# Second feed-forward of a two-layer trunk: norm and first weight tiles by token blocks of 128, with up to seven raw weight buffers

## The chip, the cores and the metric

The kernel runs on one core of a Trainium2 chip. The time is the device time of one execution in microseconds; of several runs the median is given. The engines are named as the profile names them: PE (matrix products), DVE (vector), ACT (scalar, activations), POOL (general) and SP, whose queue issues most DMAs.

## What is computed

A backbone of two layers over 256 latent tokens and 256 context tokens, 1024 features each, in float32. Layer 0 mixes tokens with an mLSTM, layer 1 with latent attention; each is followed by a gated feed-forward with a convolution over three tokens. The part around the change, for the latent tokens of layer 1, comes down to

```python
y  = attention(...) @ a_w_out                        # 256 x 1024
x3 = layer_norm(ALPHA * x2 + gate2 * y)              # per token, then * g + b
h  = x3 * (1 + scale4) + shift3
gate, up = split(h @ w_in, 2)                        # w_in: 1024 x 5632
act = silu(dwconv3(gate, conv_w) + conv_b) * up      # conv along tokens
out = layer_norm(ALPHA * x3 + gate5 * (act @ w_out))
```

## The kernel before, in words

**Arithmetic.** Each float32 operand is split into a high part in the reduced format fp32r and a low part that is the rest. A product is three matmuls (`mm3`, lines 313 to 315): high by high, high by low, low by high, summed in PSUM.

**Weights.** All weights lie in DRAM as tiles of 128 x 1024 in the order of their use (`_plan`). The class `Stream` brings them: `_load` (line 236) issues one DMA on SP's queue into a raw buffer, `_split` (line 244) makes the two parts, the cast on ACT (L257) and the subtraction on DVE (L258). There are NRAW = 3 raw buffers: a tile is loaded when an earlier one has been split. The parts go into one of NB = 3 `w` buffers ("narrow") or, for tiles marked wide, into two of the 31 buffers of 4 KB per partition of tag `u`, which activations share. `use` hands out the next tile and splits up to 8 ahead, as far as buffers and `limit` allow; `pump` raises the limit by hand; with `hold=True` a tile is kept until `unhold`.

**Order.** The Tile framework puts every operation on its engine in an order fixed before the run. The order of the code is its priority; an operation that is ready earlier by the framework's estimate may be placed ahead of others. Background work (norms) is written as generators, stepped by `tick` and finished by `drain`.

**Stages around the change.** `mla` (line 1252) computes the attention head by head and pumps the tiles of the attention output meanwhile. `outmm("aout")` multiplies the eight tiles of a_w_out; by `TAIL` the last seven are held, and the tail runs group by group: for token block 0 two groups of 512 columns, for block 1 one of 512 and two of 256 (`acc4(True)`). Then `after0` norms both blocks: `ln_rows` (L953, L954, L956 to L963, L982 to L985) makes `z`, one block after the other; `ln_T` (line 1003) transposes both blocks of `z` on PE (L1011), applies scale and shift (L1018, L1020) and splits the result into `h1` (L1023, L1024). `ln_x` later finishes x3 on DVE (L1039, L1040) and stores it for the last residual; its rows `gr` and `br` are broadcast by POOL.

`ffn_in` (line 1104) takes 22 pairs of tiles, a gate and an up tile of 128 columns of w_in each. The weights are stationary, and the 256 tokens move: 24 matmuls of 256 columns per tile. The convolution, SiLU, product and split of a pair follow (L598 to L605, L1129 to L1132). In layer 1 the first two pairs (`fin1` 0 and 1) are wide, and `pump` with QA, QB, QC = 2, 4, 6 splits them during the norm. `outmm("fout1")` with ten wide tiles and the last norm end the program.

The tags `acc` and `ar`, two buffers of 128 x 1024 each, serve the modulation vectors (L440) earlier; `ar` also holds the rope tables in the attention. The tag `s2`, 13 buffers of 128 x 512, holds residuals, gates, broadcast rows, softmax rows and small temporaries.

## Time and profile before

| what | value |
|---|---|
| median of 3 runs | 1431.02 us (1429.1 to 1434.94) |
| profiled execution | 1429.89 us, its span 1428.1 us |
| DVE, ACT busy | 980.5 us, 642.3 us |
| raw weight loads (L240, SP) | x300, 512 KB each, median 3.9 us from issue to landing |
| attention output's wide tiles on PE | 1198.8 to 1220.9 us |
| second feed-forward's first 22 pairs on PE | 1229.8 to 1357.5 us |
| granted PE clock, mean of the span | 0.996 |

All times inside the execution are counted from the span's start. The page gives each engine's busy time and share; groups of instructions by line of code; and waits, where an idle stretch of an engine is put down to whatever released it. A matmul's listed duration includes its pipeline, so the distance between starts tells what it costs. The window view gives, for a stretch of time, the busy time of each engine, the clock granted to PE (1.00 is full), the share of the DMA engines and the bytes they moved.

### The profile page before, as it was taken

The page shows a single profiled execution, that of the slowest core. Times are in us where ns is not written, and L with a number is a line of the kernel's source. Part 1 is how long each engine was busy: PE and PEld are TensorE (multiplying, and loading weights), DVE is VectorE, ACT ScalarE, POOL GpSimd, SP SyncE. Part 2 cuts the span into 40 slices and gives each one's busy share as a digit, 9 for nine tenths or more (in the row PEclk, how much of TensorE's full clock was granted, in tenths as well). Part 3 has the DMA queues.
Part 4 walks back from the last instruction along what each step waited for, and adds up shares of the span by engine and source line. Part 5 has one row for each costly group of instructions (what it writes and reads, how often), then busy time and mean ns, then how long its engine had stood idle before and what let it go on. Part 6 is the DMA issues. An engine that isn't in the chain of part 4 may idle for free.

```text
span 1428.1 us, 18819 instructions
## 1 busy us (share of the span) xinstructions
PE 1398.6 (98%) x7095; PEld 1176.5 (82%) x7095; DVE 980.5 (69%) x1437; ACT 642.3 (45%) x972; POOL 100.1 (7%) x185
## 2 busy tenths in 40 slices
PE   7999999999999999999999999999999999899997
PEld 3788888888888888888888888888887998899986
DVE  6696778885775666666787444444567888777755
ACT  6554231224334254464553333334364665555542
POOL 0010110003001010210001000000000001000000
PEclk9999999999999999999999999999999999999999
DMA  9475776777774745555635333335666315367763
GB/s 335 172 240 185 238 250 220 253 232 269 252 230 154 221 136 173 178 178 179 207 129 193 91 116 116 121 123 171 191 187 208 122 53 183 124 187 216 223 198 102
DMA packets 82827, 262.70 MB, mean 184 GB/s; under 512 B 11352, under 2 KB 19752, under 8 KB 82736
## 3 DMA queue, kind: packets, MB, share of 16 engines
q1 hardware_dynamic: 68304, 214.82, 48.2%
q0 software_dynamic: 14144, 46.17, 9.6%
q8 instruction: 55, 0.90, 0.3%
q10 hardware_dynamic: 288, 0.52, 0.1%
q14 instruction: 36, 0.29, 0.1%
HBM read 243.56 MB, written 17.91 MB: 183 GB/s over the span
## 4 chain that ended last, share of the span: by engine, by line
PE 65%; issue 18%; DMA 6%; DVE 6%; ACT 3%; POOL 2%; SPq 0%; DVEq 0%; POOLq 0%; ACTq 0%
PE fin L315 8%; PE fin L313 8%; PE fin L314 8%; PE y L314 5%; PE y L315 5%; PE y L313 5%; PE qk L315 4%; PE qk L313 4%; PE qk L314 4%; DMA raw<-in_ws 3%; DMA ar<-in_ada_w 2%; DVE wu L258 1%; PE up L313 1%; DMA xcr<-xcd 1%; PE up L315 1%
## 5 line engine op out<-in xcount | busy, mean ns | idle before, releaser
L258 DVE TENSOR_TENSOR w<-raw,w 128x1024 fp32r<-128x1024 f32 (+2 forms) x267 | 323.9, 1213 | 240.2 <-ACT w L257 239.7
L257 ACT CAST w<-raw 128x1024 fp32r<-128x1024 f32 (+2 forms) x267 | 278.6, 1045 | 437.2 <-PE tok L315 153.3
L315 PE MATMUL fin<-h,w 128*128 128x256 f32 (+1 forms) x696 | 231.6, 333 | 0.5 <-DVE w L258 0.5
L314 PE MATMUL fin<-h,w 128*128 128x256 f32 (+1 forms) x696 | 231.8, 333 | 0.0
L313 PE MATMUL fin<-h,w 128*128 128x256 f32 (+1 forms) x696 | 231.7, 334 | 0.0
L440 DVE SCALAR_TENSOR_TENSOR acc<-ar,cond,acc 128x1024 f32<-128x1024 f32 x112 | 140.6, 1279 | 36.0 <-DMA ar<-in_ada_w 35.6
L315 PEld LDWEIGHTS fin<-h,w 128*128 128x128 f32 x696 | 132.2, 190 | 13.8 <-DVE w L258 0.9
L314 PEld LDWEIGHTS fin<-h,w 128*128 128x128 f32 x696 | 132.2, 190 | 13.0 <-DVE h L1024 0.2
L313 PEld LDWEIGHTS fin<-h,w 128*128 128x128 f32 x696 | 132.0, 190 | 12.8
L313 PE MATMUL qk<-xc,w 128*128 128x512 f32 x256 | 101.1, 395 | 0.0
L313 PE MATMUL tok<-w,xm 128*128 128x512 f32 x256 | 100.4, 392 | 0.0
L315 PE MATMUL qk<-xc,w 128*128 128x512 f32 x256 | 100.1, 391 | 0.2 <-DVE w L258 0.2
L314 PE MATMUL qk<-xc,w 128*128 128x512 f32 x256 | 99.9, 390 | 0.0
L315 PE MATMUL tok<-w,xm 128*128 128x512 f32 x256 | 99.7, 389 | 0.0
L314 PE MATMUL tok<-w,xm 128*128 128x512 f32 x256 | 99.6, 389 | 0.0
L313 PE MATMUL y<-w,act 128*128 128x512 f32 (+1 forms) x212 | 80.4, 379 | 0.0
L315 PE MATMUL y<-w,act 128*128 128x512 f32 (+1 forms) x212 | 80.1, 378 | 0.0
L314 PE MATMUL y<-w,act 128*128 128x512 f32 (+1 forms) x212 | 80.1, 378 | 0.0
L258 DVE TENSOR_TENSOR wu<-raw,wu 128x1024 fp32r<-128x1024 f32 x36 | 43.9, 1222 | 21.7 <-ACT wu L257 21.3
L315 PEld LDWEIGHTS qk<-xc,w 128*128 128x128 f32 x256 | 48.1, 188 | 10.6 <-DVE w L258 0.6
L313 PEld LDWEIGHTS tok<-w,xm 128*128 128x128 f32 x256 | 48.0, 188 | 10.3
L315 PEld LDWEIGHTS tok<-w,xm 128*128 128x128 f32 x256 | 48.1, 188 | 10.1
(357 smaller groups left out, 2756.6 us busy)
## 6 DMA issues: line engine op xcount, KB each, us to landing
raw<-in_ws SPq DMA_DIRECT2D x300, 512.0 KB, 3.9
ar<-in_ada_w SPq DMA_DIRECT2D x80, 512.0 KB, 4.5
adaw<-in_ada_w SPq DMA_DIRECT2D x32, 256.0 KB, 6.5
xcd<-cv POOLq DMA_DIRECT2D x16, 256.0 KB, 3.2
od<-o POOLq DMA_DIRECT2D x16, 256.0 KB, 4.0
vd<-v POOLq DMA_DIRECT2D x16, 256.0 KB, 3.9
xcr<-xcd POOLq DMA_DIRECT2D x16, 256.0 KB, 6.7
vr<-vd POOLq DMA_DIRECT2D x16, 256.0 KB, 3.8
```

Source lines behind the costliest of these rows:

```text
L257: k.nc.scalar.copy(h[:, :cols], raw[:, :cols])
L258: k.nc.vector.tensor_sub(l[:, :cols], raw[:, :cols], h[:, :cols])
L313: mm(out, w[0], x[0], start=start, stop=False)
L314: mm(out, w[0], x[1], start=False, stop=False)
L315: mm(out, w[1], x[0], start=False, stop=stop)
L440: nc.vector.scalar_tensor_tensor(acc[j], w, s, acc[j], op0=ALU.mult, op1=ALU.add)
```

## The change

It has three parts. The four tiles of the first two pairs of layer 1 are packed another way (`fin1m`): 256 of the 1024 rows of w_in, by the 512 columns of both gate and both up tiles, so that they are the moving operand. Two of them are narrow, two wide.

The norm goes by token blocks of 128. Block 0's `ln_rows` is emitted after its last group of the attention output (`each`, called in `outmm`'s tail), its transposes and scale-and-shift (`ln_T1`) after the first group of block 1. When the attention output is done, block 1 is normed in `ln_rows`; block 0 is multiplied with the four tiles (`ffn_rows`: 24 matmuls of 512 columns, the tokens stationary); then follow block 1's `ln_T1` and its 24 matmuls. The results lie in token rows; `ffn_cols` copies them to SBUF and transposes them back, so that pairs 0 and 1 go on as before. From pair 2 on, `ffn_in` is unchanged. The residual and the gate of this norm are loaded from within `mla`, at head 6.

Raw buffers: the `Stream` keeps a ring of tags. It has the three `raw` buffers at first, from the first `fout0` tile on also the two of `acc` (five), and from the first `aout` tile on also the two of `ar` (seven); as many tiles are loaded ahead.

```diff
@@ _plan
-    for p in range(NF):
-        add(("fin1", p, 0), 1024, p < 2)
-        add(("fin1", p, 1), 1024, p < 2)
+    for c in range(4):
+        add(("fin1m", 0, c), 1024, c >= 2)
+    for p in range(2, NF):
+        add(("fin1", p, 0), 1024)
+        add(("fin1", p, 1), 1024)
@@ _pack
+        elif kind == "fin1m":
+            wi = i["ffn_w_in"][1]
+            b = _mov(np.concatenate([wi[:, :256], wi[:, F:F + 256]], axis=1), 2 * c, 2)
@@ Stream
+        keys = [x[0] for x in order]
+        self.bufs = [(0, [("raw", NRAW)] * NRAW)]
+        self.bufs.append((keys.index(("fout0", 0, 0)), self.bufs[-1][1] + [("acc", 2)] * 2))
+        self.bufs.append((keys.index(("aout", 0, 0)), self.bufs[-1][1] + [("ar", 2)] * 2))
+    def ring(self, j):
+        return [x for x in self.bufs if x[0] <= j][-1]
...
-        t = k.pool.tile([128, CW], F32, tag="raw", name="raw", bufs=NRAW)
+        j0, ring = self.ring(j)
+        tag, bufs = ring[(j - j0) % len(ring)]
+        t = k.pool.tile([128, CW], F32, tag=tag, name="raw", bufs=bufs)
...
-        while self.nl < min(self.ns + NRAW, self.n):
+        while self.nl < min(self.ns + len(self.ring(self.ns)[1]), self.n):
             self._load()
@@ K
+    def ln_T1(self, z, A, B, t, hu):
+        nc = self.nc
+        for kp in range(2):
+            pt = self.ps("zT")
+            for i in range(4):
+                k = kp * 4 + i
+                nc.tensor.transpose(pt[:, i * 128:(i + 1) * 128], z[:, k * 128:(k + 1) * 128], self.ident)
+            tmp = self.s2("zm")
+            for i in range(4):
+                k = kp * 4 + i
+                c = slice(i * 128, (i + 1) * 128)
+                if i % 2 == 0 or t == 0:
+                    nc.scalar.activation(tmp[:, c], pt[:, c], AF.Identity, bias=B[:, k:k + 1], scale=A[:, k:k + 1])
+                else:
+                    nc.vector.tensor_scalar(tmp[:, c], pt[:, c], A[:, k:k + 1], B[:, k:k + 1],
+                                            op0=ALU.mult, op1=ALU.add)
+                if i % 2:
+                    src = tmp[:, (i - 1) * 128:(i + 1) * 128].rearrange("p (k c) -> p k c", k=2)
+                    hi, lo = [hu[k // 2][:, n].rearrange("p (k c) -> p k c", k=2)[:, :, t * 128:(t + 1) * 128]
+                              for n in range(2)]
+                    nc.scalar.copy(hi, src)
+                    nc.vector.tensor_sub(lo, src, hi)
@@ outmm, tail
-                for ps, cs in pss[t]:
+                for i, (ps, cs) in enumerate(pss[t]):
                     for k, w in zip(tail, ws):
                         mms(k, w, t, ps, cs)
+                    if each is not None:
+                        each(t, i)
@@ K
+    def ffn_rows(self, ps, ws, hu, t, cs):
+        for c in cs:
+            for kk in range(2):
+                hi, lo = [hu[c][:, n, kk * 256 + t * 128:kk * 256 + (t + 1) * 128] for n in range(2)]
+                w = ws[c]
+                self.mm3(ps, (hi, lo), (w[0][:, kk * 512:(kk + 1) * 512], w[1][:, kk * 512:(kk + 1) * 512]),
+                         c == 0 and kk == 0, c == 3 and kk == 1)
+    def ffn_cols(self, pss):
+        nc = self.nc
+        rs = []
+        for ps in pss:
+            r = self.s2("fr")
+            nc.scalar.copy(r, ps)
+            rs.append(r)
+        out = []
+        for i in range(4):
+            pt = self.ps("fin")
+            for t in range(2):
+                nc.tensor.transpose(pt[:, t * 128:(t + 1) * 128], rs[t][:, i * 128:(i + 1) * 128], self.ident)
+            out.append(pt)
+        return [out[0], out[2], out[1], out[3]]
@@ ffn_in
-                if pre:
+                if pre and not isinstance(pre[0], tuple):
+                    ps = pre.pop(0)
+                elif pre:
@@ mla
+            if h == 6:
+                mid()
@@ build
-        att = k.mla(hl)
+        xg = []
+        def mid():
+            xg.extend((k.res_load(x2d, 0), k.bcast(k.gd[1, 2][0:1, :], "gate")))
+        att = k.mla(hl, mid)
...
-        xr = k.res_load(x2d, 0)
-        gate = k.bcast(k.gd[1, 2][0:1, :], "gate")
...
-        fi = [x[0] for x in order].index(("fin1", 0, 0))
-        st.limit = fi + QA
-        k.outmm("aout", range(8 - TAIL["aout"], 8), o1, pl, 0, 8, 1, True)
-        oT = None
+        fi = [x[0] for x in order].index(("fin1m", 0, 0))
+        st.limit = fi
...
-        k.bg = [after0(pl, xr, gate, 1, 2, 1, 3, h1,
-                       [x3d[0], x3d[1]])]
-        k.tick(1)
-        st.pump(fi + QB)
-        k.tick(1)
-        st.pump(fi + QC)
-        k.drain()
+        A, B = k.ln_mod_cols(2, 1, 3, 0)
+        rows = k.ln_rows(pl, *xg)
+        def each(t, i):
+            if (t, i) == (0, 1):
+                next(rows)
+                st.pump(fi + 2)
+            elif (t, i) == (1, 0):
+                k.ln_T1(k.zs[0], A, B, 0, h1u)
+                st.pump(fi + 4)
+        k.outmm("aout", range(8 - TAIL["aout"], 8), o1, pl, 0, 8, 1, True, each)
+        oT = None
+        next(rows)
+        wm = [st.use(("fin1m", 0, c), hold=True) for c in range(4)]
+        pm = [k.ps("fin") for _ in range(2)]
+        k.ffn_rows(pm[0], wm, h1u, 0, range(4))
+        st.pump(fi + 5)
+        k.ln_T1(k.zs[1], A, B, 1, h1u)
+        k.ffn_rows(pm[1], wm, h1u, 1, range(4))
+        st.unhold()
         st.limit = st.n
+        pre = k.ffn_cols(pm)
+        k.late.extend([iter(range(5)), k.ln_x(2, k.zs, [x3d[0], x3d[1]])])
         k.take_late()
-        acts = k.ffn_in(1, h1, 256, 1)
+        acts = k.ffn_in(1, h1, 256, 1, pre)
```

More of the change, by code (lines that the diff above doesn't have):

```diff
@@ L1042, in ln_x, with outmm @@
                 yield
-    def outmm(self, key, ks, act, pss, toks, nk, nt, last=False):
+    def outmm(self, key, ks, act, pss, toks, nk, nt, last=False, each=None):
         def mms(k, w, t, ps, cs):
@@ L1084, in res_load, with ffn_half @@
         return xs
-    def ffn_half(self, ps, w, hT, g):
-        gs = slice(g * 256, (g + 1) * 256)
+    def ffn_rows(self, ps, ws, hu, t, cs):
[19 more added lines that the diff above has]
+        return [out[0], out[2], out[1], out[3]]
+    def ffn_half(self, ps, w, hT, g, n=512):
+        gs = slice(g * n // 2, (g + 1) * n // 2)
         for k in range(8):
@@ L1092, in ffn_half, with ffn_pre @@
             self.mm3(ps[:, gs], (w[0][:, c], w[1][:, c]), (hi[:, gs], lo[:, gs]), k == 0, k == 7)
-    def ffn_pre(self, l, hT):
+    def ffn_pre(self, l, hT, nt, n):
         r = []
-        for n in range(NB):
-            w = self.st.use(("fin%d" % l, n // 2, n % 2), hold=True)
+        for i in range(nt):
+            w = self.st.use(("fin%d" % l, i // 2, i % 2), hold=True)
             ps = self.ps("fin")
-            self.ffn_half(ps, w, hT, 0)
+            self.ffn_half(ps, w, hT, 0, n)
             r.append((w, ps))
@@ L1112, in ffn_in @@
             for j in range(2):
-                if pre:
+                if pre and not isinstance(pre[0], tuple):
+                    ps = pre.pop(0)
+                elif pre:
                     w, ps = pre.pop(0)
-                    self.ffn_half(ps, w, hT, 1)
+                    self.ffn_half(ps, w, hT, 1, n)
                     if not pre:
@@ L1250, in mla_kv, with mla @@
         self.v1 = []
-    def mla(self, hl):
+    def mla(self, hl, mid):
         nc, st = self.nc, self.st
@@ L1490, in build @@
         h0f = lambda i: (h0[i][:, 0], h0[i][:, 1])
-        pre = k.ffn_pre(0, h0f)
+        pre = k.ffn_pre(0, h0f, NB, 512)
         k.bg = [after0(pl, xr, gate, 1, 0, 0, 3, lambda i: (h0[i][:, 0, 256:512], h0[i][:, 1, 256:512]),
```

## The prediction

> **What bounds the kernel now.** First the page: its engine line shows PE busy for 98% of the span, so time can only be won where PE waits or is slow, and such places are few.

> ```profile
> PE 1398.6 (98%) x7095; PEld 1176.5 (82%) x7095; DVE 980.5 (69%) x1437; ACT 642.3 (45%) x972; POOL 100.1 (7%) x185
> ```

> Second, the waits in three stretches: around the second feed-forward's start (1200 to 1250 us), the end of the first feed-forward's output (1072 to 1092) and the last output projection (1382 to 1408). Each line tells who waited for whom: us in total, times, longest.

> ```profile
> PE zT L1011 <- DVE z L984: 5.0, 1, 5.0
> PE y L313 <- ACT wu L257: 0.7, 1, 0.7
> ...
> PEld y L314 <- DVE wu L258: 1.7, 3, 0.9
> ...
> ACT wu L257 <- DMA raw<-in_ws: 11.2, 9, 1.8
> ...
> PE y L314 <- DVE wu L258: 0.8, 1, 0.8
> ```

> PE waits once for a norm (the transposes `zT` need `z`), and three times for split weights; behind the last of these ACT waits nine times for a raw load. Third, PE's timeline at the seam; each row is a start, a duration, the line, and in brackets the idle time before it.

> ```profile
> 1207.37 0.50 PE L313 MATMUL y<-wu,oT 128*128 128x512 f32 x1 [0.69 <-ACT wu L257]
> ...
> 1220.82 0.28 PE L315 MATMUL y<-wu,oT 128*128 128x256 f32 x1
> 1221.18 0.44 PE L1011 MATMUL zT<-ident,z 128*128 128x128 f32 x2
> 1221.89 0.44 PE L1011 MATMUL zT<-ident,z 128*128 128x128 f32 x2 [0.27 <-ACT z L985]
> 1227.34 2.82 PE L1011 MATMUL zT<-ident,z 128*128 128x128 f32 x12 [5.01 <-DVE z L984]
> 1229.81 0.56 PE L313 MATMUL fin<-h,wu 128*128 128x256 f32 x1
> ...
> 1242.30 0.28 PE L313 MATMUL fin<-h,w 128*128 128x256 f32 x1
> ```

> The attention output ends at 1220.9; the four tiles of pairs 0 and 1 run from 1229.8 to 1242.3. Fourth, the stage windows; the seventh number group is PE's granted clock.

> ```profile
> 1224.00:1225.00 1.00, 0.00 (x0) 0.00 (x0) 1.00 (x3) 0.00 (x0) 0.00 (x0) 0.97 0.00 0
> 1225.00:1226.00 1.00, 0.00 (x0) 0.00 (x0) 0.97 (x3) 0.00 (x0) 0.00 (x0) 0.50 0.90 168
> ...
> 1230.00:1231.00 1.00, 1.00 (x6) 1.00 (x6) 1.00 (x4) 1.00 (x5) 0.00 (x0) 0.50 0.00 0
> 1231.00:1232.00 1.00, 1.00 (x8) 1.00 (x7) 1.00 (x3) 1.00 (x4) 0.00 (x0) 0.62 0.00 0
> 1232.00:1234.00 2.00, 2.00 (x19) 2.00 (x18) 2.00 (x6) 0.88 (x3) 0.00 (x0) 1.00 0.00 0
> ```

> PE's quiet stretch also halves its clock from about 1225.0 to 1231.8 (6.8 us), so the first `fin` matmuls start 0.21 us apart instead of 0.12. From 1235 to 1365 PE is never idle.

> **The unit prices.** From starts in PE's timeline: a matmul with 512 moving columns every 0.2275 us (1202.66, 1202.89, 1203.12 ...), with 256 every 0.12 (1216.02, 1216.14 ...), a 128-column transpose every 0.06 at full clock. A split of a weight tile takes 1.05 us on ACT (L257) and 1.22 on DVE (L258).

> **Part 1, the seam.** Before, from 1220.82 to 1242.30 is 21.5 us. In it stand 16 transposes (1.0) and 4 x 24 matmuls of 256 columns (11.5); the remaining 9.0 us is waiting and half clock.

> After, w_in's first four tiles are the moving operand, 512 columns wide, and a token block of 128 is stationary: 2 x 24 matmuls x 0.2275 = 10.9 us. Block 0's chain runs while PE still works on block 1's share of the attention output: 7 tiles x 3 x 0.2275 = 4.8 us for its first group, then 2 x 2.5 us for the 256-column ones. The pure chain, from the last `y` group of block 0 to `z`, is three DVE passes (0.6 each, start to start), aggregate 0.2, square root 0.3, two tiny ones 0.3, and two ACT passes 1.5: 4.1 us, under the 4.8. Then 8 transposes (0.5) and the scale-and-shift: by length, L1018's 256 columns take 0.56 and L985's 512 take 0.81, so 128 take an estimated 0.44 (0.35 start to start); 8 of these and 4 casts of 0.3 are 4.0 us on ACT, under the 5.0 us of `y` that follow. So block 0 costs PE its transposes alone if the order holds. Block 1's norm tail (`y` end to `z` was 6.4 us, of which two splits at 1222.80 and 1224.28 took 2.4 in between) stands beside block 0's 24 `fin` matmuls of 5.5 us: hidden without those splits, 1 us late with them.

> Left bare is block 1's scale-and-shift. At 1106.67 transposes began and ACT's L1018 began at 1107.26: 0.6; then 0.44, the cast 0.40 and some 0.15 to the first matmul: 1.6, of which 0.5 is transposing, so **1.1 idle** (bounds 0.8 and 3: the latter with one split, 1.05 and 1.22, ahead on ACT or DVE). The later pieces come every 0.7 us, and PE takes 1.4 per pair.

> Rows must be turned back: two ACT copies (0.60, as for `PT`) and 8 transposes (0.5). PE need not wait for the second copy, since pair 2's first matmuls are ready (its tile is split ahead, in the third `w` buffer): 0.3 taken, bounds 0 and 1.1 (copy 0.6, two handovers, the transposes of one pair).

> So after: last `y` 0.1 + 10.9 + 16 transposes 1.0 + 1.1 + 0.3 = 13.4, and 8 transposes (0.5) ahead of it. The gain is 21.5 - 13.4 - 0.5 = 7.6.

> The stall at 1206.29 goes too: the next matmul came 1.08 later instead of 0.23, the one after 0.1 late. ACT had waited 3.25 us for that raw tile, which seven buffers hold early: +1.0 (bounds 0 and 1.0).

> Against it I set 0.8 for block 0's transposes waiting in PE's fixed order. Before, block 0's chain took 10.7 us (1211.17 to 1221.84), not 4.1, because three splits stood among its steps on DVE and two casts and a table load (1.28) on ACT. The bounds are 0 and 6.0 (1210.2 + 10.7 = 1220.9, against PE's arrival at 1214.9). I take a value near 0, since the casts that stood in the way had come late from DMA (2.28 and 2.48 us of waiting at 1212.28 and 1215.82) and all five tiles are now in SBUF: they can be split from 1203 to 1210. Seam: 7.6 + 1.0 - 0.8 = **7.8**.

> [...]

> **Part 2, raw buffers.** Five from the first output projection of the feed-forward (`acc` is last read at 783 us), seven from the attention output (`ar`'s rope tables are read until about 1150). A raw load takes 4.5 us to land; with ACT and DVE that is 6.8 us for a round of three, 2.26 per tile (ACT's casts from 1383.68 to 1404.35 go by 2.30, nine steps). The same 512 KB needs 1.9 us at the 280 GB/s of 1125 to 1130, so there is room, but the main effect is that five or seven tiles lie ready when a burst of wide splits begins, and these then go at DVE's 1.2. In 1080 to 1090 PE's starts are late by 2.4 us in sum; with five, the sixth wide tile is split at about 1085, when it is needed: **2.2** (bounds 0 and 3.6, with the 1.2 us at 1105.4 gone too). At 1405.45 one start came 1.26 later instead of 0.23: **1.0** (bounds 0 and 1.0). Elsewhere PE is not short of weights: 0.

> **At no cost.** `mid` issues six loads of residual and gate (0.55 us each on POOL) earlier; before, they were issued at 1174 to 1184 already, when buffers came free, and the same buffers are held. POOL's queue has only the next norm's rows behind them. ln_mod_cols (three tiny DVE operations) moves ahead of the matmuls. ln_x is five ticks later; its 8 DVE passes (5.5 us) hide in the feed-forward, where DVE is busy 90.5 of 130 us, and x3d is read back only from 1292. The number of weight loads is unchanged. Half the w_in tiles become narrow, in two of the three `w` buffers; the first comes free a quarter into block 1's matmuls, 4 us before pair 2 starts; without that cover, one split (2.3 us) would be bare.

> **Sum.** 7.8 + 2.2 + 1.0 = 11.0 from the profiled execution's 1429.9 (span 1428.1 and 1.8 around it): 1418.9. That run was 1.1 under the median of the runs, 1431.0, so I say **1420**.

> **Rivals.**
> (a) Norm in the way: PE's order puts block 0's transposes before `z` is there, or block 1's splits stand in its chain. For: the 10.7 us above. Against: the tiles are early now. The 6.0 us in place of 0.8 gives 1425; half of it 1422.5.
> (b) The ring gives nothing, because the 16 DMA engines, not the buffers, set 2.26 per tile (they were 0.91 busy at 280 GB/s once). Against: their share is 0.68 from 1382 to 1406. Without 1.0, 2.2 and 1.0: 1424. So too if buffers of the `u` tag, not raw ones, hold the splits; that is the case in which the change doesn't do what it says.
> (c) Slower: all five splits stand ahead of block 0's chain on DVE (4.1 + 5 x 1.22 + a load of the square root's table 1.28 + two casts 2.1 = 13.6 us), so PE stops at 1214.9 for 8.9 us in mid-projection, and the clock halves as it did after 1222 (6.8 us at half is 3.4 lost). 8.9 - 0.8 + 3.4 = 11.5 eats the 11.0, and a second halving at block 1 costs 3.4 more: 1435. It decides from a chain of some 13 us on; 10.7 was seen.
> [...]

> **Chances.** Forecast, 1416 to 1422: 0.50. (a) 0.22, (b) 0.13, (c) 0.15, a third of it slow enough to count. Differences under 0.5% (7.2 us) are about what a measurement of this kernel cannot tell from no change. Under 1423.9 is faster: the forecast, most of (a), half of (b): 0.72. Within: 0.19. Slower: 0.09. The range that leaves out 2 in 10 is 1415 to 1428: below by the stall at 1105 and no wait of block 0, above by (a), (b) and the mild half of (c).

> **What would show it.** Right: no PE idle over 2 us between 1195 and 1240, clock 1.00 there, pair 2 starting some 13.4 us after the last `y`; no ACT wait on raw after 1382; `y` without gaps at 1080 to 1090. Wrong: `zT` waiting for L982 or L985 in the middle of `y`; clock 0.50 in the seam; `fin` waiting for `w` at pair 2 or 3; DVE's L258 between L953 and L963.

## The result and the profile after

The median of 22 runs was 1429.08 us (1424.10 to 1432.91), that of the kernel before, over 22 runs in turn with it, 1431.65 (1429.10 to 1434.94): a ratio of 0.9983, interval 0.9975 to 0.9992, or some 2.5 us (1.1 to 3.6). Forecast were 1420 us and a gain of 11.

The profiled execution took 1432.91 us, its span 1431.1. On PE, ACT and DVE both kernels run the same instructions until after 969.6 us, where `fout0` starts in the trace of before; the trace of after gets there at 976.0. The traces of the other kernels lie between (970.2 to 974.1), so these 6.4 us are most likely chance of the early stages, and everything below is compared from that point on. The page's engine line:

```profile
PE 1400.3 (98%) x7055; PEld 1176.4 (82%) x7055; DVE 980.0 (68%) x1437; ACT 644.1 (45%) x982; POOL 100.0 (7%) x185
```

It hardly moved. PE's timeline, cut into stages between matmuls that both kernels have, shows where time went (us; "ring" and "all edits" are experiments told below):

| from, to | before | after | ring alone | all edits |
|---|---|---|---|---|
| first `y` of fout0, first `dq` | 153.31 | 150.83 | 150.69 | 150.97 |
| first `dq`, last `o` (attention) | 78.47 | 79.90 | 78.48 | 78.47 |
| last `o`, last `y` (attention output) | 19.44 | 19.58 | 18.43 | 19.43 |
| last `y`, last `fin` (seam, feed-forward) | 136.56 | 135.61 | 133.59 | 129.39 |
| last `fin`, last `y` of fout1 | 62.27 | 61.06 | 61.06 | 61.06 |
| last `y`, end of DVE's last pass | 4.83 | 4.84 | 4.83 | 4.84 |
| sum | 454.88 | 451.82 | 447.08 | 444.16 |

Behind the last row the span goes on for 3.65 us before and 3.3 in the other three. Each column is one trace; over the eleven traces with the ring the first row is 150.5 to 152.1, over the three without it 153.0 to 153.4. The feed-forwards' output projections gained a little more than forecast (2.5 and 1.2 beside 2.2 and 1.0). The attention lost 1.4: PE waits there for the last softmax rows, transposed (`PT`), the first line before and the second after:

```profile
PE o L314 <- DVE PT L319: 0.4, 1, 0.4
...
PE o L328 <- ACT PT L333: 1.3, 1, 1.3
```

The seam, which was to give 8.1 in that stretch (21.5 less 13.4), gave 0.95. PE's waits there, 1203 to 1253 us:

```profile
PE zT L1051 <- DVE z L999: 2.8, 1, 2.8
PE fin L328 <- ACT h L1065: 1.3, 1, 1.3
```

Then PE's timeline of the same place (start, duration, line, in brackets the idle time before it):

```profile
1226.35 0.28 PE L330 MATMUL y<-wu,oT 128*128 128x256 f32 x1
1226.47 0.40 PE L328 MATMUL fin<-w,h 128*128 128x512 f32 x1
...
1231.71 0.39 PE L330 MATMUL fin<-wu,h 128*128 128x512 f32 x1
1234.92 1.09 PE L1051 MATMUL zT<-ident,z 128*128 128x128 f32 x8 [2.82 <-DVE z L999]
1237.34 0.79 PE L328 MATMUL fin<-w,h 128*128 128x512 f32 x1 [1.33 <-ACT h L1065]
1237.93 0.63 PE L329 MATMUL fin<-w,h 128*128 128x512 f32 x1
1238.36 0.63 PE L330 MATMUL fin<-w,h 128*128 128x512 f32 x1
...
1246.16 0.36 PE L328 MATMUL fin<-h,w 128*128 128x256 f32 x1
```

Block 0 went as meant: its 24 matmuls follow the last `y` without a gap. Block 1's `z` came 8.4 us after the last `y`, and the cover is 5.5. From 1237.9 on the matmuls start 0.43 us apart, not 0.23, and the window view shows why (the seventh group is PE's clock):

```profile
1234.00:1236.00 2.00, 1.08 (x8) 0.86 (x8) 0.78 (x3) 1.21 (x3) 0.00 (x0) 1.00 0.11 45
1236.00:1238.00 2.00, 0.67 (x3) 0.56 (x3) 1.50 (x4) 2.00 (x7) 0.00 (x0) 0.66 0.00 0
1238.00:1240.00 2.00, 2.00 (x6) 1.59 (x5) 1.08 (x4) 0.60 (x2) 0.00 (x0) 0.50 0.00 0
1240.00:1242.00 2.00, 2.00 (x7) 1.44 (x6) 0.62 (x1) 1.35 (x2) 0.00 (x0) 0.50 0.00 0
1242.00:1244.00 2.00, 2.00 (x7) 1.63 (x6) 0.95 (x2) 0.92 (x1) 0.00 (x0) 0.63 0.36 33
```

The first 14 steps of block 1's matmuls took 6.26 us (1237.34 to 1243.60). DVE's timeline tells why `z` was late:

```profile
1220.02 0.16 DVE L978 SCALAR_TENSOR_TENSOR nm<-mv,rs 128x1 f32<-128x1 f32 x1
1223.26 0.42 DVE L1066 TENSOR_TENSOR h<-zm,h 128x256 fp32r<-128x256 f32 x1 [3.08 <-ACT h L1065]
1224.26 0.42 DVE L1066 TENSOR_TENSOR h<-zm,h 128x256 fp32r<-128x256 f32 x1 [0.58 <-ACT h L1065]
1225.26 0.43 DVE L1066 TENSOR_TENSOR h<-zm,h 128x256 fp32r<-128x256 f32 x1 [0.58 <-ACT h L1065]
1226.06 0.43 DVE L1066 TENSOR_TENSOR h<-zm,h 128x256 fp32r<-128x256 f32 x1 [0.37 <-ACT h L1065]
1227.01 2.36 DVE L273 TENSOR_TENSOR wu<-raw,wu 128x1024 fp32r<-128x1024 f32 x2 [0.53 <-ACT wu L272]
1229.29 1.02 DVE L968 TENSOR_TENSOR z<-y,gate 128x512 f32<-128x512 f32 x2
...
1234.33 0.54 DVE L999 TENSOR_SCALAR z<-z,mv,rs 128x512 f32<-128x512 f32 x1
```

DVE stands idle for 3.08 us, because the next in its order is a subtraction of block 0 that waits for ACT. Behind it stand the other subtractions, the two wide splits and then all passes of block 1 (L968), though block 1's first 512 columns were ready some 5.9 us before the last `y` (1216.82 against 1222.69 in the first experiment). In the code, `next(rows)` for block 1 stands behind `ln_T1` of block 0 and `pump(fi + 4)`. In this trace DVE kept to that order: it idled for 3.08 us, to 1223.26, though the last matmul of block 1's first 512 columns had started at 1220.07, and their first pass began at 1229.29.

**Theory T** is therefore: the order on DVE makes block 1's `z` late by 2.8 us, and the wait brings the halved clock with it. Its rivals: the chain is too long in itself, or the clock falls for another reason.

### The profile page after: what moved, and what is told of

The parts are those of the page before. It is cut to its first block, busy times and chain, and to the rows that moved or that the text cites. A ratio compares the mean times of both kernels' runs of the same rounds, so it can differ in the third digit from the quotient of the medians.

```text
span 1431.1 us, 18733 instructions
## 1 busy us (share of the span) xinstructions
PE 1400.3 (98%) x7055; PEld 1176.4 (82%) x7055; DVE 980.0 (68%) x1437; ACT 644.1 (45%) x982; POOL 100.0 (7%) x185
## 4 chain that ended last, share of the span: by engine, by line
PE 69%; issue 18%; DMA 5%; DVE 4%; ACT 2%; POOL 2%; SPq 0%; DVEq 0%; POOLq 0%; ACTq 0%
PE fin L330 8%; PE fin L328 8%; PE fin L329 8%; PE y L329 6%; PE y L330 6%; PE y L328 6%; PE qk L330 4%; PE qk L328 4%; PE qk L329 4%; DMA ar<-in_ada_w 2%; DMA raw<-in_ws 2%; DMA xcr<-xcd 1%; PE up L328 1%; PE up L330 1%; PE up L329 1%
## 5 line engine op out<-in xcount | busy, mean ns | idle before, releaser
L330 PEld LDWEIGHTS fin<-h,w 128*128 128x128 f32 x696 | 132.2, 190 | 13.6 <-DVE w L273 0.9
L330 PEld LDWEIGHTS qk<-xc,w 128*128 128x128 f32 x256 | 48.5, 189 | 12.9 <-DVE w L273 2.8
L328 PEld LDWEIGHTS qk<-xc,w 128*128 128x128 f32 x256 | 48.5, 189 | 10.0
L329 PEld LDWEIGHTS qk<-xc,w 128*128 128x128 f32 x256 | 48.5, 190 | 9.7
L328 PEld LDWEIGHTS tok<-w,xm 128*128 128x128 f32 x256 | 48.0, 188 | 10.3
```

Of the source, the lines that this page charges most:

```text
L328: mm(out, w[0], x[0], start=start, stop=False)
L329: mm(out, w[0], x[1], start=False, stop=False)
L330: mm(out, w[1], x[0], start=False, stop=stop)
```

## Experiments on the seam

**Block 1's passes earlier.** After the change, with `ln_rows` yielding after each group of block 1, and stepped as these groups end:

```diff
+                if step and t and i < len(pss[t]) - 1:
+                    yield
...
             elif (t, i) == (1, 0):
+                next(rows)
                 k.ln_T1(k.zs[0], A, B, 0, h1u)
                 st.pump(fi + 4)
+            elif (t, i) == (1, 1):
+                next(rows)
```

> After the change, with one edit: block 1's norm passes are emitted group by group as its groups of the attention output end, and so stand ahead of block 0's subtractions in DVE's fixed order. Theory T (DVE's order made block 1's z late: z came 8.4 us after the last y, the cover is 5.5, then the wait and the wait for the scale-and-shift halved PE's clock): the wait of zT for z falls from 2.8 to under 1 us, the granted clock stays 1.00 in the seam, and the time falls by 4 to 6 us, to some 1424. Rival R1 (block 1's chain is long by itself, or block 0's transposes now wait in its place): the wait stays over 2 us or moves to block 0, and the time is within 1 us of the change's 1429.

Measured: 1424.68 us, ratio 0.9947 (0.9934 to 0.9961). PE's only wait in the seam:

```profile
PE fin L328 <- ACT h L1067: 1.3, 1, 1.3
```

The clock stayed up through this wait:

```profile
1228.00:1230.00 2.00, 1.31 (x10) 0.95 (x9) 0.57 (x2) 1.43 (x4) 0.00 (x0) 1.00 0.90 365
1230.00:1232.00 2.00, 1.36 (x6) 1.03 (x7) 1.63 (x6) 1.90 (x6) 0.00 (x0) 1.00 0.06 23
```

From the last `y` to pair 2 it is 13.9 us instead of 19.8, and the 14 steps took 3.45 instead of 6.26. T holds, by its numbers.

**The wide splits earlier.** `pump(fi + 4)` moved from behind `ln_T1` of block 0 to (0, 1), ahead of its norm:

```diff
             if (t, i) == (0, 1):
                 next(rows)
-                st.pump(fi + 2)
+                st.pump(fi + 4)
             elif (t, i) == (1, 0):
                 k.ln_T1(k.zs[0], A, B, 0, h1u)
-                st.pump(fi + 4)
```

> After the change, with one edit: the two wide splits of fin1m stand ahead of block 0's norm chain instead of between block 0's subtractions and block 1's passes. Theory T: 2.4 us of DVE leave the way of block 1's z, so its wait falls from 2.8 to about 0.5 us, the idle time of PE is too short for the clock to fall, and the time is 3 to 5 us under the change's 1429. Rival R1: the splits only move the wait to block 0's transposes (zT then waits in the middle of y), and nothing is won. Rival R2 (it is block 0's subtractions, not the splits): the wait stays over 2 us.

Measured: 1423.69 us, 0.9942 (0.9929 to 0.9955). The wait for `z` fell to 0.9, the clock stayed at 1.00, and the seam to pair 2 took 15.1. The first rival didn't come about: block 0's transposes waited for nothing. With the splits out of its way `z` is still 0.9 late, with three of block 0's four subtractions still ahead of its first pass in DVE's order. In this trace the attention took 81.5 us instead of 79.9, because the clock fell to 0.50 there (last section).

**Both** of these edits.

> After the change, with both edits: block 1's passes group by group, and the two wide splits ahead of block 0's norm chain. Theory T: no wait for z at block 1, full clock, 5 to 6 us under the change's 1429, the best of the three. Rival R1: block 0's z, later by the two splits, takes back what block 1 gives: 1427 to 1429, with zT waiting before block 1's second group of y.

Measured: 1423.76 us, 0.9947 (0.9932 to 0.9962); the seam to pair 2 took 13.9. It was not the best of the three: their intervals overlap, and only the traces say that the passes are worth 1.2 us more than the splits and that both together add nothing to the passes alone.

**Work in the gap.** After the change, with matmuls that nobody reads:

```diff
         k.ffn_rows(pm[0], wm, h1u, 0, range(4))
         st.pump(fi + 5)
+        idle = k.ps("idle")
+        for _ in range(12):
+            nc.tensor.matmul(idle, h1u[3][:, 0, 256:384], wm[3][0][:, 512:1024], start=True, stop=True)
         k.ln_T1(k.zs[1], A, B, 1, h1u)
```

> After the change, with extra work: 12 matmuls of 512 columns, whose results nobody reads, stand on PE between block 0's 24 fin matmuls and block 1's transposes, where PE stood idle for 2.8 us. They take 12 x 0.2275 = 2.7 us, the length of that wait. Theory T (about 2.6 us of the seam's loss are the clock, halved because PE was idle): the clock stays at 1.00 from 1232 to 1245 and the time is 2 to 3 us under the change's 1429 although work was added. Rival R3 (the clock falls for another reason, or the loss is the waiting alone): the time is the same as the change's or up to 2.7 us above.

Measured: 1426.40 us, 0.9961 (0.9946 to 0.9975). With 2.7 us of work added, the seam to pair 2 took 17.0 us instead of 19.8: 2.8 less. The wait for block 1's first cast was as long as after the change (1.3 us), with full clock:

```profile
1232.00:1234.00 2.00, 1.36 (x10) 0.86 (x8) 0.73 (x3) 1.64 (x4) 0.00 (x0) 1.00 0.02 6
1234.00:1236.00 2.00, 1.20 (x5) 0.95 (x6) 1.63 (x5) 2.00 (x6) 0.00 (x0) 1.00 0.00 0
```

So 2.8 us of the loss are the clock's, and it falls because PE stood idle before. The other traces agree: three more kernels in which `zT` of block 1 waits for 2.8 us or longer (the change without its ring 3.9, narrow splits kept behind 3.4, loads at their old place 2.8) show the halved clock in the seam (mean of the span 0.995 to 0.996), the eight in which it waits for 0.9 at most don't (0.997 to 0.999).

## Experiments on the parts

**The ring alone**: the kernel before with the change's lines in `Stream` (`bufs`, `ring`, and their use in `_load` and `_split`).

> The kernel before, with the ring of raw buffers alone (five from the first fout0 tile, seven from the first aout tile). Theory: the ring gives what the change's trace shows in the first feed-forward's output (2.5 us) and in the second's (1.2), and up to 1.0 where the aout tile came late, so 1427 to 1428 beside 1431.7; the attention stays at 78.5 us, since the ring has no narrow tiles there to split early. Rival A (the ring itself, by its transfers or its order, costs the attention its 1.4 us): the stretch from the first dq to the last o is 79.9 here too, and the time 1428 to 1430. Rival B (the first feed-forward's 2.5 us are chance): no gain there.

Measured: 1425.38 us, 0.9946 (0.9931 to 0.9960). One part of the change, alone, is faster than the whole. It gained more than expected: beside 2.6, 1.0 and 1.2 us another 3.0 in the seam. Its first `zT` waits less there than before (5.0):

```profile
PE zT L1021 <- DVE z L994: 3.3, 1, 3.3
```

The tiles were in SBUF early, so one split, begun ahead of the last `y`, stood among the last norm's passes instead of two behind it (`zT` went on 4.0 us after the start of the last `y`, 6.5 before), and the clock was halved for 3.4 us instead of 6.8. The attention lost nothing, against rival A.

**The change without its ring**:

```diff
-        self.bufs.append((keys.index(("fout0", 0, 0)), self.bufs[-1][1] + [("acc", 2)] * 2))
-        self.bufs.append((keys.index(("aout", 0, 0)), self.bufs[-1][1] + [("ar", 2)] * 2))
```

> The change without its ring (three raw buffers throughout; packing and norm by blocks as in the change). Theory: the first feed-forward's output takes 153.3 us again instead of 150.8 and the second's 62.3 instead of 61.1, so 3.7 us are lost; the fin1m tiles come too late from DMA to be split in the softmax, so the attention takes 78.5 instead of 79.9 and 1.4 come back: 1431 to 1433, no better than the kernel before. It shows whether norm by blocks alone is worth anything as it is ordered. Rival: the late tiles also delay the seam, and the time is over 1434.

Measured: 1437.13 us, 1.0030 (1.0018 to 1.0042): slower than before, and worse than expected; the rival was right. `fout0` took 153.0 and `fout1` 62.3 again. ACT's waits, 1205 to 1235 us:

```profile
ACT w L270 <- DMA raw<-in_ws: 7.6, 3, 6.4
ACT wu L270 <- DMA raw<-in_ws: 2.5, 1, 2.5
```

ACT stood 6.4 us at the cast of a tile still in DMA, ahead of block 0's square root; block 0's `zT` waited 1.6 us in mid-projection and block 1's 3.9. The attention was still 79.8, which spoke against the narrow splits as its cause.

**Both order edits without the ring.**

> Block 1's passes group by group and the wide splits ahead of block 0's chain, but without the ring (three raw buffers throughout). It asks whether the norm by blocks, well ordered, is worth anything by itself. Theory T alone: about 5 us under the change without its ring, which took 1437, so 1432, the time of the kernel before. Theory L (the norm by blocks needs the ring: without it ACT, in its fixed order, stands 6.4 us at the cast of a narrow tile that is still in DMA, ahead of block 0's square root, and the wide casts ahead of block 0's chain will wait there as well): zT waits in mid-projection for 2 to 6 us, and the time is 1434 to 1438.

Measured: 1427.29 us, 0.9966 (0.9955 to 0.9978). Both theories were wrong, by 4.7 us and more: `zT` waited only 0.2 us, block 0's first `fin` matmul 0.8 for its cast, and the seam to pair 2 took 15.7. Well ordered, the norm by blocks is worth something without a ring; as the change ordered it, it costs.

## Experiments on the attention

**Narrow splits kept behind it.** After the change, with the splits of the two narrow `fin1m` tiles bound to the place in which they are emitted, and emitted when the attention is done:

```diff
+        if key[0] == "fin1m" and not wide:
+            k.tc.keep_in_program_order(c)
+            k.tc.keep_in_program_order(s)
...
-            if (t, i) == (0, 1):
+            if (t, i) == (0, 0):
+                st.pump(fi + 2)
+            elif (t, i) == (0, 1):
                 next(rows)
-                st.pump(fi + 2)
```

> After the change, with one edit: the casts and subtractions of the two narrow fin1m tiles are kept, on their engines, behind everything emitted before them, and emitted when the attention is done, so that they can't stand in the softmax. Theory N (these two splits, 2 x 1.05 us on ACT and 2 x 1.2 on DVE, cost the attention its 1.4 us): the stretch from the first dq to the last o falls from 79.9 to 78.5 and the time by about 1.4 us to 1427.5, unless the splits now delay block 0's z. Rival A (the loads of residual and gate, or the ring's transfers, cost it): the stretch stays at 79.9.

Measured: 1429.56 us, 0.9980 (0.9970 to 0.9991). The stretch took 79.8, so theory N fell as it stood:

```profile
PE o L328 <- ACT PT L333: 1.0, 1, 1.0
PE o L329 <- DVE PT L334: 0.3, 1, 0.3
```

**The loads at their old place.** After the change, with `mid()` called when the attention is done:

```diff
-            if h == 6:
-                mid()
...
+        mid()
         pl = k.acc4(True)
```

> After the change, with one edit: the loads of residual and gate are emitted after the attention, as in the kernel before, instead of at head 6. Theory M (these six loads, 5 us earlier than before, hold buffers of tag s2 that the last heads' softmax rows then wait for, and this, not the narrow splits, is the attention's loss): the stretch from the first dq to the last o is 78.5 us instead of 79.9, the 1.3 us wait of o for PT goes, and the time is some 1.3 under the change's. Rival (block 0's norm now has its residual late, or the loss comes from the narrow splits or the order alone): the stretch stays at 79.8, or zT waits.

Measured: 1428.45 us, 0.9979 (0.9965 to 0.9992). The stretch took 80.3; theory M fell too, and block 0's `zT` now waited 0.8 us in mid-projection:

```profile
PE o L328 <- ACT PT L333: 1.5, 1, 1.5
PE o L329 <- DVE PT L334: 0.2, 1, 0.2
```

**All edits but one of these.** Both order edits, narrow splits kept behind, and the copies of `ffn_cols` kept behind block 1's casts:

```diff
-            nc.scalar.copy(r, ps)
+            self.tc.keep_in_program_order(nc.scalar.copy(r, ps))
```

> Block 1's passes group by group and the wide splits ahead of block 0's chain, with two further edits: the narrow fin1m splits kept behind the attention, and the copies of ffn_cols kept behind block 1's casts. Theories T and N: 1.4 us in the attention and some 0.5 us of PE's 1.3 us wait for block 1's first cast are added to that version's gain, so 1421 to 1422.5, about 10 us under the kernel before. Rival: all five splits now stand before block 0's z, zT waits in mid-projection, and the gain of the attention is lost again: 1423 to 1425.

Measured: 1421.71 us, 0.9922 (0.9909 to 0.9934). The attention took 79.8 again, and block 0's `zT` waited 0.2 us. The copies behind the casts made the seam to pair 2 13.6 instead of 13.9. The same with the old loads in place of the kept splits:

> Block 1's passes group by group, the wide splits ahead of block 0's chain, the copies of ffn_cols kept behind block 1's casts, and the loads of residual and gate emitted after the attention (the narrow splits left free, since keeping them behind the attention gave nothing there). By theories T and M: the gain of the first two (8.0 us under the kernel before), plus 1.3 in the attention, plus 0.3 at block 1's first cast, so about 9.6 under the kernel before, 1422. By the rival to M: 1423.5.

Measured: 1422.82 us, 0.9936 (0.9923 to 0.9948); the attention took 79.9. The time lies between the 1422 of the theories and the 1423.5 of the rival and decides nothing; the 79.9 is the third sign that neither cause is alone.

**Both at once**, with the two order edits and the copies kept behind: the table's last column, "all edits".

> Block 1's passes group by group, the wide splits ahead of block 0's chain, the copies of ffn_cols kept behind block 1's casts, and both attention edits at once: the narrow fin1m splits kept behind the attention, and the loads of residual and gate emitted after it. Theory S (either of the two is enough to disorder the last softmax rows, so that each edit by itself gave nothing: 79.8 and 80.3 us): with both gone, the stretch from the first dq to the last o is 78.5 us, as in the kernel before and in the ring alone, and the time is 1.3 under the version that has only the narrow splits kept back: about 1420.4. Rival (something else in the change disorders the attention, or the residual now comes too late for block 0's norm): the stretch stays at 79.8 or zT waits longer, and the time is 1421.5 to 1423.

Measured: 1421.90 us, 0.9921 (0.9904 to 0.9938). The attention took 78.47, as before the change. PE's waits from 1185 to 1245 us; of the attention's only the one is left that the kernel before has as well (0.4):

```profile
PE fin L328 <- ACT h L1067: 1.0, 1, 1.0
PE o L329 <- DVE PT L334: 0.4, 1, 0.4
```

Theory S holds, in the one trace of it: either edit of the change is enough to disorder the last softmax rows. The 1.3 us don't show in the medians (1421.90 here, 1421.71 with the kept splits alone), whose intervals are wider than that. By which buffer or estimate the early loads change the order was not tried, and stays open.

## Why the prediction was wrong

The sum of its gains was reached, but by another kernel: with all edits the stages gain 454.88 - 444.16 = 10.7 us, forecast 11.0, and no stage is off by more than 1 us. It missed the order in which the change itself puts the work. Of the 7.9 us by which the change's stages (3.1) fell short of it, 7.1 are the seam's and 1.4 the attention's; the three projections did some 0.6 better.

- **The step that failed**: "Block 1's norm tail ... stands beside block 0's 24 `fin` matmuls of 5.5 us: hidden without those splits, 1 us late with them." The sum took "hidden" and set this wait at nothing. The step priced the two splits in the chain, and let the chain begin when `y` ends. What stands ahead of it on DVE, block 0's four subtractions and their waits for ACT, was not counted, though the diff puts `next(rows)` behind them. PE waited 2.8 us for `z`, not 0 or 1; without the splits in the way it was 0.9, not 0 (second experiment).
- **No clock in that step.** The sum sets nothing for the clock behind block 1's 1.1 us of idling, an assumption of its author. In the seam that wait left it at 1.00 (1.3 us idle, first and fourth experiment); behind one of 2.8, with 1.3 after it, it was 0.50. The clock cost 2.8 (6.26 - 3.45). That 1.3 us always keep it is not so: in the attention of two traces it fell behind such a wait (last section).
- **Block 1's first cast**: from the first transpose to the first matmul 1.6 us were forecast, 2.4 came; the copy L1143 stood ahead of the cast, and with it behind, it took 2.0. The three make 6.4 of the 7.1 us by which the stretch from the last `y` to the last `fin` missed its 128.5 (13.4, and 115.1 behind it as before); the rest, 0.7, is the excess of the stretch behind pair 2, in which the turning back stands.
- **Block 0**: 0.8 us of waiting was set, 0 came. Rival (a) in the form it was given (block 0's transposes) was wrong, in the form "block 1's splits stand in its chain" half right.
- **The 8 transposes ahead of the last `y`**: 0.5 forecast, 1.0 measured (18.43 to 19.43), since each group of four also slows the 256-column matmuls next to it (starts 0.17 and 0.20 us apart instead of 0.12).
- **The aout stall**: right, 1.0 (19.44 to 18.43), but the transposes take it back.
- **Part 2**: 2.2 and 1.0 forecast, 2.5 and 1.2 measured, right. What was not seen is that the ring takes 3.0 us out of the old seam by itself; the prediction gave these to the norm by blocks.
- **At no cost**: "`mid` issues six loads ... earlier", and the narrow tiles split ahead. The attention, costed at 0, lost 1.4 us by either.
- **Rival (b)**, the ring gives nothing, was the most wrong: alone the ring gains 0.5%, and without it the change as built loses 0.3%. It is not the only way to gain: the norm by blocks, well ordered, gains 0.3% without it. **Rival (c)** described the kernel without its ring: PE stopped in mid-projection, though for 1.6 us and not 8.9.

## What to carry to other kernels

Where each engine runs a fixed order, as DVE did here (3.08 us idle ahead of work that was ready), a piece of work is hidden only if it also stands early enough in the order of every engine it needs: go through the queue of each, from the emission in the code, before calling a chain covered. Measure the parts of a change apart: here one part alone was faster than the whole, since another lost on what it gained. Move work into another stage only after a look at what it reorders there, loads and "early" splits too.

## What the runs showed of the hardware

The half clock came in several lengths. From the windows' mean clock it is worked out as 6.8 us after the change (0.66 and 0.63 at its ends: 1236.65 to 1243.5), as before the change (1224.94 to 1231.76), and 3.4 us with the ring alone, whose PE idled for 3.3 us in one piece; without the ring it lasted 10.2 (mean clock of its span 0.995). After the change the idle stretches were 2.82 and 1.33 us with eight transposes between them, and the clock fell to 0.50, while 0.9 and 1.3 us with eight transposes between (the second experiment) left it at 1.00.

How long a wait is doesn't decide alone. The attention of the change and of the first four experiments has the same wait of 1.3 us in the same place and order. In the second and the fourth experiment's traces the clock was halved behind it for 3.4 us, and the attention took 81.5 us; in the other three it stayed at 1.00, and the attention took 79.9. The second experiment, a window behind that wait:

```profile
1194.00:1195.00 1.00, 1.00 (x7) 1.00 (x7) 1.00 (x2) 0.00 (x0) 0.00 (x0) 0.50 0.60 143
```
